# Stores and reloads of a streaming softmax kernel on two issuing queues instead of one

## The chip, the core and the metric

The kernel runs on one core of one Trainium2 chip. The metric is the device time of one execution in microseconds (us), taken as the median of several runs. Beside the times there is a profile of one execution: a trace of each engine's instructions and of the DMA transfers, and a page that sums it up. The engines that matter here are VectorE (DVE in the profile), ScalarE (ACT) and SyncE (SP). SyncE computes nothing; it issues DMAs. A name with a q behind it (SPq, ACTq, DVEq) is the instruction sequencer of that engine, which waits on semaphores and issues DMAs.

## What is computed

```python
B, H, S = 2, 8, 2112
rel = pos[:, None] - pos[None, :]
bias = rel_bias[:, np.clip(rel, -16, 16) + 16]      # H x S x S
logits = logits + bias[None]
exp = np.exp(logits - logits.max(axis=-1, keepdims=True))
return exp / exp.sum(axis=-1, keepdims=True)
```

It is a row softmax over a 2 x 8 x 2112 x 2112 float32 tensor, with a bias that depends only on the distance between row and column. All 285 MB of the input are read once and all 285 MB of the output are written once.

## The kernel before, in words

The tensor has B·H·S = 33792 rows of 2112 numbers. Each of the 128 partitions owns 264 rows that follow one another in memory (`ROWS`). They are worked through in 44 **chunks** of 6 rows (`R = 6`), so that one chunk is 128 partitions x 12672 numbers, 6336 KB. Four buffers `X[0]` to `X[3]` (`NBUF`) take the chunks in turn, chunk n in buffer n mod 4, and everything happens in place in the buffer. In the text below, L(n) is the load of chunk n, S(n) its store.

Each engine has its own program, and they meet only through semaphores:

- **VectorE** (loop at L191): for each chunk `add` (L162) waits for the load (`ld[b]`), then adds the bias row by row and takes the row's minimum of the negated sum, one instruction per row, and counts up `added`. Then `scale` (L180) waits in two halves of three rows for the exponentials (`expd`), takes reciprocals, multiplies each row and counts up `scaled`. `add` of the next chunk starts only after `scale` of this one, since it is one program.
- **ScalarE** (loop at L197): `exps` (L171) waits for `added` row by row and does one exponential with its sum per row.
- **SyncE** issues every load and every large store (L86 to L92, L203 to L214). It begins with six one-row loads of chunk 0, then L(1), L(2), L(3). Then comes S(0), and a loop whose step for chunk j is: wait until chunk j+1 is scaled, issue S(j+1), wait until S(j) has landed (`st[b]`), issue L(j+4) into the buffer that has come free. The last three chunks are stored behind the loop, the last one in two halves of three rows. `take` (L73) is the wait on a semaphore that also counts it down again.

Loads and stores thus stand in one queue, in the order S(j+1), L(j+4), S(j+2), L(j+5). One load or store is spread over the core's 16 DMA engines, eight partitions to each.

The set-up before the loops (L96 to L156) builds the bias lookup `M` once; the change does not touch it. ScalarE issues one small DMA there, for the bias table (L97).

Of the kernel before, what the change touches and what calls it, by code (L numbers as in the profile page):

```python
# [11 lines left out]
ENG = mybir.EngineType  # L12
# [3 lines left out]
def kernel(  # L16
# [6 lines left out]
    nc = tc.nc  # L23
# [5 lines left out]
    ROWS = B * H * S // P  # L29
    PB = S // ROWS  # L30
    assert ROWS * P == B * H * S and PB * ROWS == S and PB == H == 8
    R = 6
    NBUF = 4
    STEP = R * NBUF
    N = ROWS // R
    HALF = R // 2
# [6 lines left out]
    X = [io.tile([P, R * S], FP32, tag=f"X{b}", name=f"X{b}") for b in range(NBUF)]  # L43
# [9 lines left out]
    def view(t, offset, dims):  # L53

        return bass.AP(tensor=t.tensor, offset=t.offset + offset, ap=[[list(t.ap[0])[0], P]] + dims)

    def rows(t, j, n):

        return bass.AP(tensor=t.tensor, offset=t.offset + j * S, ap=[[ROWS * S, P], [1, n * S]])

    with tc.tile_critical(no_gpsimd_drain=True):
        ld = [nc.alloc_semaphore(f"ld{b}") for b in range(NBUF)]
        st = [nc.alloc_semaphore(f"st{b}") for b in range(NBUF)]
# [9 lines left out]
        def take(eng, sem, n):  # L73
            eng.wait_ge(sem, n).then_inc(sem, -n)  # L74


        def load(j, b):
            nc.sync.dma_start(out=X[b][:, :], in_=rows(logits, j, R)).then_inc(ld[b], 16)

        def store(j, b, s0=0, n=R):  # L80
            take(nc.sync, scaled, n)
            nc.sync.dma_start(
                out=rows(out, j + s0, n), in_=X[b][:, s0 * S : (s0 + n) * S]
            ).then_inc(st[b], 16)


        for r in range(R):
            nc.sync.dma_start(
                out=X[0][:, r * S : (r + 1) * S], in_=rows(logits, r, 1)
            ).then_inc(ld[0] if r == R - 1 else pre, 16)  # L90
        for n in range(1, NBUF):
            load(n * R, n)  # L92

# [2 lines left out]
            out=rbB,  # L98
            in_=bass.AP(tensor=rel_bias.tensor, offset=rel_bias.offset, ap=[[0, P], [1, H * W]]),
# [27 lines left out]
        for m, op in ((eq, ALU.is_equal), (gt, ALU.is_gt), (le, ALU.is_le), (lt, ALU.is_lt)):  # L127
# [4 lines left out]
            out=view(F, 0, [[W, H], [1, W]]), in0=view(F, 0, [[W, H], [1, W]]),  # L132
# [9 lines left out]
            out=view(F, 0, [[W, PB], [1, W]]), in0=view(F, SC + 2 * PB, [[1, PB], [0, W]]),  # L142
# [7 lines left out]
            out=view(M, U, [[ROWS, PB], [1, W]]), in0=view(F, 0, [[W, PB], [1, W]]),  # L150
            in1=view(F, SC + 8 * PB, [[1, PB], [0, W]]), op=ALU.add))
        then(v.tensor_copy(out=view(M, U + W, [[ROWS, PB], [1, ROWS - W]]),  # L152
                           in_=view(F, SC + 7 * PB, [[1, PB], [0, ROWS - W]])))
# [14 lines left out]
                    op0=ALU.add, op1=ALU.min, accum_out=nmax[:, r : r + 1],  # L168
                ).then_inc(added, 1)

        def exps(b):  # L171
            for r in range(b * R, (b + 1) * R):
                x = X[b][:, (r - b * R) * S : (r - b * R + 1) * S]
                take(nc.scalar, added, 1)
                nc.scalar.activation(  # L175
                    out=x, in_=x, func=EXP, scale=-1.0, bias=nmax[:, r : r + 1],
                    accum_out=tot[:, r : r + 1],
                ).then_inc(expd, 1)

        def scale(b):  # L180
            for r0 in range(b * R, (b + 1) * R, HALF):
                take(v, expd, HALF)
                v.reciprocal(out=rec[:, r0 : r0 + HALF], in_=tot[:, r0 : r0 + HALF]).then_inc(inv, 1)  # L183
                take(v, inv, 1)
                for r in range(r0, r0 + HALF):
                    x = X[b][:, (r - b * R) * S : (r - b * R + 1) * S]
                    v.tensor_scalar_mul(out=x, in0=x, scalar1=rec[:, r : r + 1]).then_inc(scaled, 1)  # L187
# [3 lines left out]
        with nc.Fori(0, ROWS - STEP + 1, STEP, engines=[ENG.DVE]) as j:  # L191
            strip(j)
            take(v, dve, 1)
            for b in range(NBUF):
                add(b)
                scale(b)
        with nc.Fori(0, ROWS // STEP, 1, engines=[ENG.Activation]):  # L197
            for b in range(NBUF):
                exps(b)

        store(0, 0)  # L203
        with nc.Fori(0, ROWS - 2 * STEP + 1, STEP, engines=[ENG.SP]) as j:
            for b in range(NBUF):
                store(j + (b + 1) * R, (b + 1) % NBUF)
                take(nc.sync, st[b], 16)
                load(j + (b + NBUF) * R, b)
        for n in range(N - NBUF + 1, N - 1):
            store(n * R, n % NBUF)  # L210
        store((N - 1) * R, (N - 1) % NBUF, 0, HALF)
        store((N - 1) * R, (N - 1) % NBUF, HALF, R - HALF)
        for b in range(NBUF):
            take(nc.sync, st[b], 32 if b == (N - 1) % NBUF else 16)  # L214


# [28 lines left out]
```

## Time and profile before

| | us |
|---|---|
| time, median of 3 runs (lowest to highest) | 1329.75 (1329.24 to 1329.9) |
| span of the profiled execution, first to last instruction | 1327.7 |
| median less span (what lies around the span) | 2.05 |
| VectorE busy | 976.6 |
| ScalarE busy | 575.2 |
| bytes moved by DMA | 571.11 MB |

The profiled execution's own device time is not listed apart from its span; the three times lie within 0.66 us of each other, so the span with 2.05 us around it is used for it. How to read the views: the page gives each engine's busy time and share, what the DMA queues moved, and for each kind of DMA issue the median time from issue to landing. The timeline has one line per instruction (or per run of alike instructions): its start, its duration, its engine and program line, the operation with the tensors it writes and reads, and behind "x" how many. The view by windows gives busy times of each engine between two points in time, and as its last two columns the mean busy share of the 16 DMA engines and the rate in GB/s. The view of the waits says which engine waited for what, how long in total, how often, and the longest.

### The profile page before, as it was taken

What the parts mean: (1) busy time and instruction counts of PE and PEld (TensorE: products, weight loads), DVE (VectorE), ACT (ScalarE), POOL (GpSimd) and SP (SyncE); (2) the same over time, 40 slices, a digit from 0 to 9 for tenths busy, and PEclk for the clock granted to TensorE, in tenths of its full rate; (3) what the DMA queues carried; (4) which work ended last, traced back from release to release, by engine and by line L of the source; (5) the groups of instructions that cost most, each with busy time, mean ns of one, the idle gap of its engine ahead of it and who ended that gap; (6) DMA issues with size and microseconds to landing.
All of it is one profiled execution on the core that took longest, in us unless ns stands there. A gap on an engine that the chain in (4) does not pass through costs nothing. (4 is left out here: it accounts for less than half of the span.)

```text
span 1327.7 us, 2454 instructions
## 1 busy us (share of the span) xinstructions
DVE 976.6 (74%) x911; ACT 575.2 (43%) x539; POOL 0.4 (0%) x6
## 2 busy tenths in 40 slices
DVE  6999667777777776687778777677877776687772
ACT  2564333444444343345444333444444343335440
POOL 0000000000000000000000000000000000000000
DMA  9999999999999999999999999999999999999998
GB/s 392 431 428 437 435 420 437 435 434 425 435 437 434 428 435 434 435 429 429 438 438 432 426 438 437 437 425 437 437 437 425 435 440 437 428 432 438 437 426 359
DMA packets 13683, 571.11 MB, mean 430 GB/s; under 512 B 1521, under 2 KB 1649, under 8 KB 1649
## 3 DMA queue, kind: packets, MB, share of 16 engines
q1 hardware_dynamic: 13536, 570.96, 99.6%
q10 hardware_dynamic: 144, 0.14, 0.1%
q14 instruction: 3, 0.02, 0.0%
HBM read 285.61 MB, written 285.47 MB: 430 GB/s over the span
## 5 line engine op out<-in xcount | busy, mean ns | idle before, releaser
L166 DVE CUSTOM_DVE_ANT_0 X<-X,F 128x2112 f32<-128x2112 f32 x264 | 605.2, 2354 | 301.3 <-DVEq L74 301.3
L175 ACT ACTIVATE X<-X,nmax 128x2112 f32<-128x2112 f32 x264 | 541.7, 2052 | 539.3 <-ACTq L74 517.6
L187 DVE TENSOR_SCALAR X<-X,rec 128x2112 f32<-128x2112 f32 x264 | 332.4, 1315 | 13.2
L175 ACT ACT_TABLE_LOAD x11 | 14.1, 1283 | 183.3 <-ACTq L74 183.3
L175 ACT ACTIVATION_READ_ACCUMULATOR X<-X,nmax 128x1 f32 x264 | 49.2, 186 | 0.0
L160 DVE COPY F<-M 128x2135 f32 x11 | 26.1, 2374 | 6.3 <-DVEq L74 6.3
L166 DVE DVE_READ_ACCUMULATOR2_ANT nmax<- 128x1 f32 x264 | 21.7, 82 | 0.0
L183 DVE RECIPROCAL rec<-tot 128x3 f32<-128x3 f32 x88 | 14.9, 170 | 0.0
L131 DVE TENSOR_TENSOR F<-F 128x264 f32<-128x264 f32 x1 | 0.4, 434 | 4.7 <-DMA F<-in_rel_bias_dram 4.7
L152 DVE COPY M<-F 128x1848 f32<-128x1848 f32 x1 | 2.1, 2077 | 0.0
L118 DVE TENSOR_SCALAR ip<-ip 128x8 int32<-128x8 int32 x1 | 0.2, 173 | 1.3 <-POOL ip L102 1.3
L135 DVE TENSOR_REDUCE rbS<-F 128x33 f32<-128x264 f32 x1 | 0.6, 610 | 0.0
L149 DVE TENSOR_TENSOR M<-F 128x264 f32<-128x264 f32 x1 | 0.4, 441 | 0.0
L141 DVE TENSOR_TENSOR F<-F,rbS 128x264 f32<-128x264 f32 x1 | 0.4, 425 | 0.0
L128 DVE TENSOR_SCALAR F<-F 128x8 f32<-128x8 f32 x4 | 0.4, 166 | 0.0
L154 DVE COPY M<-rbS 128x247 f32<-128x247 f32 x1 | 0.4, 408 | 0.0
L139 DVE TENSOR_SCALAR F<-F,rbS 128x8 f32<-128x8 f32 x1 | 0.2, 231 | 0.0
L145 DVE SCALAR_TENSOR_TENSOR F<-F,rbS 128x8 f32<-128x8 f32 x1 | 0.2, 225 | 0.0
L140 DVE TENSOR_SCALAR F<-F,rbS 128x8 f32<-128x8 f32 x1 | 0.2, 222 | 0.0
L146 DVE SCALAR_TENSOR_TENSOR F<-F,rbS 128x8 f32<-128x8 f32 x1 | 0.2, 219 | 0.0
L124 DVE TENSOR_TENSOR F<-ip 128x8 f32<-128x8 int32 x1 | 0.2, 167 | 0.0
L121 DVE TENSOR_TENSOR F<-ip 128x8 f32<-128x8 int32 x1 | 0.2, 166 | 0.0
(9 smaller groups left out, 1.2 us busy)
## 6 DMA issues: line engine op xcount, KB each, us to landing
X<-in_logits_dram SPq DMA_DIRECT2D x43, 6336.0 KB, 44.6
out_dram<-X SPq DMA_DIRECT2D x43, 6336.0 KB, 52.6
X<-in_logits_dram SPq DMA_DIRECT2D x6, 1056.0 KB, 12.1
out_dram<-X SPq DMA_DIRECT2D x2, 3168.0 KB, 21.1
F<-in_rel_bias_dram ACTq DMA_DIRECT2D x1, 132.0 KB, 6.2
```

The lines of the kernel that those rows point to most:

```text
L128: then(v.tensor_scalar(out=m, in0=dp, scalar1=0.0, scalar2=None, op0=op))
L131: then(v.tensor_tensor(out=view(F, 0, [[W, H], [1, W]]), in0=view(F, 0, [[W, H], [1, W]]), in1=view(F, SC + 3 * PB, [[1, H], [0, W]]), op= ...
L135: then(v.tensor_reduce(out=rbS[:, :], in_=view(F, 0, [[1, W], [W, H]]), axis=mybir.AxisListType.X, op=ALU.add))
L141: then(v.tensor_tensor(out=view(F, 0, [[W, PB], [1, W]]), in0=view(F, SC + 2 * PB, [[1, PB], [0, W]]), in1=view(rbS, W - 1, [[0, PB], [-1, ...
L149: then(v.tensor_tensor(out=view(M, U, [[ROWS, PB], [1, W]]), in0=view(F, 0, [[W, PB], [1, W]]), in1=view(F, SC + 8 * PB, [[1, PB], [0, W]] ...
L152: then(v.tensor_copy(out=view(M, U + W, [[ROWS, PB], [1, ROWS - W]]), in_=view(F, SC + 7 * PB, [[1, PB], [0, ROWS - W]])))
L154: then(v.tensor_copy(out=M[:, 0:U], in_=low.to_broadcast([P, U])))
L160: v.tensor_copy(out=F[:, :], in_=M[:, bass.ds(ROWS - STEP - j, FW)]).then_inc(dve, 1)
L166: v.tensor_tensor_reduce(out=x, in0=x, in1=F[:, STEP - 1 - r : STEP - 1 - r + S], scale=-1.0, scalar=BIG, op0=ALU.add, op1=ALU.min, accum_ ...
L175: nc.scalar.activation(out=x, in_=x, func=EXP, scale=-1.0, bias=nmax[:, r : r + 1], accum_out=tot[:, r : r + 1],).then_inc(expd, 1)
L183: v.reciprocal(out=rec[:, r0 : r0 + HALF], in_=tot[:, r0 : r0 + HALF]).then_inc(inv, 1)
L187: v.tensor_scalar_mul(out=x, in0=x, scalar1=rec[:, r : r + 1]).then_inc(scaled, 1)
```

## The change

All loads but the first two chunks' move from SyncE's queue to ScalarE's. ScalarE issues L(2) and L(3) right behind the first row's exponential of chunk 0. In its loop the step for chunk j is: the exponentials of chunk j+1, then a wait until S(j) has landed, then the issue of L(j+4). SyncE's loop is left with the stores alone: wait until chunk j is scaled, issue S(j). The last two chunks (42 and 43) are stored in halves, where before only chunk 43 was. VectorE's program is the same in both kernels.

```diff
-        def load(j, b):
-            nc.sync.dma_start(out=X[b][:, :], in_=rows(logits, j, R)).then_inc(ld[b], 16)
+        def load(eng, j, b):
+            eng.dma_start(out=X[b][:, :], in_=rows(logits, j, R)).then_inc(ld[b], 16)
...
-        for n in range(1, NBUF):
-            load(n * R, n)
+        load(nc.sync, R, 1)
...
-        def exps(b):
-            for r in range(b * R, (b + 1) * R):
+        def exps(b, first=0, last=R):
+            for r in range(b * R + first, b * R + last):
...
-        with nc.Fori(0, ROWS // STEP, 1, engines=[ENG.Activation]):
+        exps(0, 0, 1)
+        for n in range(2, NBUF):
+            load(nc.scalar, n * R, n)
+        exps(0, 1, R)
+        with nc.Fori(0, ROWS - 2 * STEP + 1, STEP, engines=[ENG.Activation]) as j:
             for b in range(NBUF):
-                exps(b)
-        store(0, 0)
+                exps((b + 1) % NBUF)
+                take(nc.scalar, st[b], 16)
+                load(nc.scalar, j + (b + NBUF) * R, b)
+        for n in range(N - NBUF + 1, N):
+            exps(n % NBUF)
         with nc.Fori(0, ROWS - 2 * STEP + 1, STEP, engines=[ENG.SP]) as j:
             for b in range(NBUF):
-                store(j + (b + 1) * R, (b + 1) % NBUF)
-                take(nc.sync, st[b], 16)
-                load(j + (b + NBUF) * R, b)
-        for n in range(N - NBUF + 1, N - 1):
+                store(j + b * R, b)
+        for n in range(N - NBUF, N - 2):
             store(n * R, n % NBUF)
-        store((N - 1) * R, (N - 1) % NBUF, 0, HALF)
-        store((N - 1) * R, (N - 1) % NBUF, HALF, R - HALF)
+        for n in range(N - 2, N):
+            store(n * R, n % NBUF, 0, HALF)
+            store(n * R, n % NBUF, HALF, R - HALF)
         for b in range(NBUF):
-            take(nc.sync, st[b], 32 if b == (N - 1) % NBUF else 16)
+            take(nc.sync, st[b], 32 if b >= NBUF - 2 else 16)
```

## The prediction

> **What bounds the kernel now.** I read the page first, then the waits, then SyncE's timeline, then windows. The page says that no compute engine is near full and that the DMA engines are:
>
> ```profile
> span 1327.7 us, 2454 instructions
> DVE 976.6 (74%) x911; ACT 575.2 (43%) x539; POOL 0.4 (0%) x6
> ...
> DMA packets 13683, 571.11 MB, mean 430 GB/s; under 512 B 1521, under 2 KB 1649, under 8 KB 1649
> q1 hardware_dynamic: 13536, 570.96, 99.6%
> ...
> X<-in_logits_dram SPq DMA_DIRECT2D x43, 6336.0 KB, 44.6
> out_dram<-X SPq DMA_DIRECT2D x43, 6336.0 KB, 52.6
> X<-in_logits_dram SPq DMA_DIRECT2D x6, 1056.0 KB, 12.1
> out_dram<-X SPq DMA_DIRECT2D x2, 3168.0 KB, 21.1
> ```
>
> One queue holds the DMA engines for 99.6% of the span. Its 94 issues (43 + 43 + 6 + 2) make 13536 packets, 144 each: on each of 16 engines 8 rows and one more packet for the semaphore. The waits point the same way: SyncE waits nearly throughout, and VectorE's largest wait is for loads.
>
> ```profile
> SPq L74 <- SPq L74: 1273.1, 87, 36.9
> ...
> DVE X L166 <- DVEq L74: 301.3, 41, 8.8
> ```
>
> SyncE's timeline gives the beat. L78 is a load, L82 a store; each load from the one at 81.12 on is issued at the moment at which a store has landed on all 16 engines.
>
> ```profile
> 4.36 1.74 SPq L78 DMA_DIRECT2D X<-in_logits_dram  x3
> 43.07 22.23 SPq L82 DMA_DIRECT2D out_dram<-X  x2
> 81.12 0.36 SPq L78 DMA_DIRECT2D X<-in_logits_dram  x1
> ...
> 126.28 0.35 SPq L78 DMA_DIRECT2D X<-in_logits_dram  x1
> 133.23 0.34 SPq L82 DMA_DIRECT2D out_dram<-X  x1
> ...
> 579.19 0.35 SPq L78 DMA_DIRECT2D X<-in_logits_dram  x1
> ...
> 1237.05 0.35 SPq L78 DMA_DIRECT2D X<-in_logits_dram  x1
> ```
>
> From 126.28 to 579.19 there are 15 periods of 30.19 us, from 579.19 to 1237.05 there are 22 of 29.90 us. The late beat is steady, and one load and one store take half of it each, 14.95 us, if they cost the same. When a load is issued, the load before it and one store are still queued, about 30 us of work, and it lands 44.6 us later. So the queue never runs dry: this kernel is bound by transfers, end to end. Windows confirm it and show the edges:
>
> ```profile
> 0.00:2.00 2.00, 0.63 (x5) 0.00 (x0) 0.42 (x6) 1.00 0.00 2
> ...
> 126.00:428.00 302.00, 219.09 (x203) 130.02 (x123) 0.00 (x0) 1.00 1.00 433
> ...
> 934.00:1237.00 303.00, 225.61 (x209) 134.80 (x128) 0.00 (x0) 1.00 1.00 434
> ...
> 1320.00:1328.00 8.00, 0.00 (x0) 0.00 (x0) 0.00 (x0) 1.00 0.27 114
> ```
>
> The last two columns are the DMA engines' mean busy share and the rate. Early and late windows differ by about 1 GB/s in the mean over 16 engines, though the beat differs by 0.29 us in 30 (1%). So the early loss falls on some engines only, and the beat follows the slowest. Its sum is 15 x 0.29 = 4.35 us. The last window shows the same lag at the end: 0.27 x 8 = 2.2 us of work per engine, while the last store lands over 6 us into it. By the late beat the loss has stopped, once some engines trail the others. My reading is that it arises where all engines turn from load to store together; the rows don't prove the cause.
>
> **The change, part by part.** Bytes: both kernels move the same 571.11 MB in the same rows, so the 29.90 us of a load and a store stay, if two queues are served at the rate of one. What could differ is whether an engine ever has nothing to do, and what a row costs.
>
> *Hold on ScalarE.* The new wait for S(j) stands ahead of L(j+4) and of all later exponentials. Behind it on ScalarE are exps(j+2), behind those VectorE's scaling of chunk j+2, then S(j+2). Its price is read from the first chunk (a row of exponentials, the scaling, the next chunk's first add) and the second:
>
> ```profile
> 24.94 2.06 ACT L175 ACTIVATE X<-X,nmax 128x2112 f32<-128x2112 f32 x1
> ...
> 37.10 0.19 ACT L175 ACTIVATION_READ_ACCUMULATOR X<-X,nmax 128x1 f32 x1
> 38.87 0.17 DVE L183 RECIPROCAL rec<-tot 128x3 f32<-128x3 f32 x1
> 39.19 3.78 DVE L187 TENSOR_SCALAR X<-X,rec 128x2112 f32<-128x2112 f32 x3
> 42.88 2.35 DVE L166 CUSTOM_DVE_ANT_0 X<-X,F 128x2112 f32<-128x2112 f32 x1
> ...
> 56.76 2.06 ACT L175 ACTIVATE X<-X,nmax 128x2112 f32<-128x2112 f32 x1
> ...
> 64.58 2.35 DVE L166 CUSTOM_DVE_ANT_0 X<-X,F 128x2112 f32<-128x2112 f32 x1
> ```
>
> Six exponentials in a row take 37.29 - 24.94 = 12.35 us; from the reciprocal to the store's issue is 43.07 - 38.87 = 4.2 us; a DMA issue is 0.35 us (SyncE's, taken for ScalarE's). So S(j+2) can be issued 0.4 + 12.35 + 4.2 = 17.0 us after S(j) has landed. The adds of chunk j+2 are out of the way by then: chunk j+1 was released one beat earlier, so VectorE was free at 17.0 - 29.9 = -12.9 us, and adds last 13.9 us (42.88 to 56.76). At S(j)'s landing the engines still have S(j+1) and the new L(j+4), 14.95 + 14.95 = 29.9 us. S(j+2) comes 12.9 us before they run dry, whatever order the two queues are served in. Cost: 0 on the path; if that cover were gone, each us past 29.9 would be a us per beat.
>
> *Loads.* L(j+4) is needed when VectorE gets to chunk j+4, 29.9 + 17.0 = 46.9 us after S(j)'s landing. Alone it takes 14.95 us, beside a store at half rate 29.9 us, plus what is left of L(j+3). It is 17 us early. VectorE's 301.3 us of waiting for loads shrink and turn into waits for exponentials, which is worth nothing, as VectorE doesn't set the end.
>
> *Start.* L(2) and L(3) are issued behind the first exponential, at 24.94 to 27.0 us, instead of at 5 us. L(1) covers that:
>
> ```profile
> L78 SPq DMA_DIRECT2D X<-in_logits_dram x2: 537/600/664, 4.4 to 4.9; - x2
> ...
> DMA to landing us min/median/max: 31.2/38.6/46.0
> ```
>
> L(1), issued at 4.4, lands at 35.6 us, over 8 us after the new issue. Two issues on ScalarE take 0.8 us and delay S(0) by at most that, while L(2) and L(3) run. Cost 0; gain 0, since S(0) merely shares with loads that ran ahead of it before. SyncE's loop loses its waits and load issues, also worth 0: it was waiting.
>
> *Tail.* Loads no longer stand behind stores, so less store work may be left to cover the last compute. Count from S(39)'s landing, which releases L(43) and exps(41). Compute: S(41) at 17.0; chunk 42 takes 64.58 - 42.88 = 21.7, so 38.7; chunk 43 another 21.7, so its second half is issued at 60.4 and its first 4 us before, at 56.4 us. Transfers: L(43), S(40), S(41), S(42), 4 x 14.95 = 59.8 us. An issue at 0.92 to 0.97 moved nothing until 2.00 in the first window, so about 1 us to the first byte. Margin 59.8 - 57.4 = 2.4 us: no gap, but thin. Halving chunk 42 adds one issue of 0.34 us off the path and gains nothing: engines get to S(42) at 3 x 14.95 = 44.9 us, when it has been whole since 38.7. Halving chunk 43 was there before.
>
> *What a row costs with two queues at once.* No row of before shows this. Served a whole transfer at a time, an engine turns from load to store once a period as now; served row by row, 8 times. One turn costs the slowest engine 0.29 us (early beat less late beat) or 0 (late beat). The late beat holds for 22 of 37 periods, and with engines out of step, as they would be with mixed queues; I take 0. Below nothing it can go as far as the early loss goes away, -4.35 us. Above, 7 more turns in 43 periods are 301 turns: at 0.29 us, 87 us; at the mean engine's early loss (433 against 434 GB/s is about 0.07 us a period), 21 us.
>
> On the order of service, the Trainium skill (DMA: Bandwidth & Descriptors, "Queues, rings and completion order") says that each DMA engine goes round-robin between queues with work and changes only at packet boundaries. That would be the row-by-row end, eight turns: the sum stays at zero price and is 1351 us at 0.07 us. No row here shows two bulk queues together.
>
> Sum: 1327.7 + 2.05 around it + 0 + 0 + 0 + 0 = 1329.75, the median of the runs; I say **1329.5**.
>
> **The rivals.**
> (A) *The lag never builds.* Two queues break up the common turn from load to store, the early beat becomes 29.90 too: 1329.75 - 4.35 = **1325.4**. For: the loss exists and ended without any rest in traffic. Against: the engines start in step in both kernels, so it may build up all the same. Against A stands the Trainium skill (DMA: Bandwidth & Descriptors, "Issuing engines are not separate DMA queues"): several issuing engines save only issue time; by that alone the time stays 1329.75, and the steady 434 GB/s agrees that there is little to win.
> (B) *Turns cost in every period.* Place: the DMA engines, wherever both queues hold rows. Price as above, 21 us by the mean engine: **1351**, up to 1417. It decides against the kernel from 2.7 us / 301 = 9 ns a turn. For: early beats show turns that cost. Against: 22 later periods show turns at 0.
> (C) *A gap in the tail.* If compute there takes over 2.4 us longer than counted (the hold delays chunk 41, say), the engines stand idle ahead of S(43). With 3 to 6 us over, **1333**.
> That the split does nothing since the queue was always full is my forecast itself.
>
> **How the numbers follow.** Forecast 40% (1327.2 to 1332.3, its own range), A 25% (1323.5 to 1327), B 28% (1333 to 1417), C 7% (1332.5 to 1336). A measurement of this kernel can tell about 0.2%, 2.66 us, from no change. Faster 0.25 is A; same 0.40 the forecast; slower 0.35 is B and C. From 1323.5 to 1352 holds all but half of B (14%) and a few per cent at the low end.
>
> **What would show it.** On the new page: two queues with about half the bytes each, the rate still 434 GB/s in mid-run windows, stores landing some 45 us and loads 30 us or more after issue. The beat between stores: 29.9 us throughout speaks for A, 30.2 early and 29.9 late for the forecast, over 30.3 all along for B. ScalarE should wait at its line 74 for stores, VectorE for exponentials rather than loads. For C, a window behind the last load with a DMA share well below 1 ahead of the last drain. If the DMA share falls in mid-run, my count of the hold on ScalarE is wrong.

## The result, and the profile after

The changed kernel takes 1335.68 us (median of 22 runs, 1327.48 to 1337.58) against 1330.12 us of the kernel before (22 runs beside it on the same chip, 1328.92 to 1333.13). The ratio is 1.0027, 95% interval 1.0015 to 1.0039: slower by about 0.3%, and clear of the noise. (The ratio is worked out from the single runs, so it isn't the quotient of the two medians, 1.0042.) What is new is the scatter. The old kernel's runs lie within 4.2 us, the new one's within 10.1 us, with 5 of 22 under 1331 us and 13 over 1334 us. The profiled run is one of the long ones: 1337.58 us, span 1335.8 us, so 1.8 us lie around the span. Ratios, here and below, leave out runs more than 1.5% above the fastest of their kernel.

The page of the changed kernel, the lines that answer to those shown of before:

```profile
span 1335.8 us, 2464 instructions
DVE 981.2 (73%) x911; ACT 545.8 (41%) x529; POOL 0.4 (0%) x6
...
DMA packets 13826, 571.11 MB, mean 428 GB/s; under 512 B 1536, under 2 KB 1664, under 8 KB 1664
q1 hardware_dynamic: 7632, 298.45, 51.8%
q10 hardware_dynamic: 6192, 272.64, 47.3%
...
X<-in_logits_dram ACTq DMA_DIRECT2D x42, 6336.0 KB, 37.5
out_dram<-X SPq DMA_DIRECT2D x42, 6336.0 KB, 42.6
```

The change did what it says: two queues with about half of the bytes each. A load and a store take 37 and 43 us from issue to landing. That alone doesn't show how the queues are served, since waiting in one queue made it 45 and 53 us before. The packets do: the kept trace lists each DMA packet (one for each row; a row is one partition's 50,688 bytes of a chunk) with its queue, start and duration, and on one engine a packet starts within a few ns of the end of the one before. So the neighbours on an engine can be found: 2886 load rows are followed by a store row, 3025 store rows by a load row. The engines serve both queues together, row by row. The Trainium skill (DMA: Bandwidth & Descriptors, "Queues, rings and completion order") has each engine go round between its queues, and these packets agree. The waits of the changed kernel:

```profile
ACT X L174 <- ACTq L74: 721.4, 42, 19.3
DVE rec L182 <- DVEq L74: 304.5, 80, 7.8
...
DVE X L165 <- DVEq L74: 5.5, 12, 2.1
```

VectorE waited 301.3 us for loads before; now it waits 304.5 us for exponentials and 5.5 us for loads. Idle time has moved from one wait to another. It isn't what makes the time: the same transfers without any computation take as long (e4 below). The end shows what does. Windows of the changed kernel:

```profile
934.00:1237.00 303.00, 226.36 (x206) 126.79 (x123) 0.00 (x0) 1.00 1.00 432
1308.00:1313.00 5.00, 4.79 (x7) 2.97 (x4) 0.00 (x0) 1.00 0.09 41
1314.00:1328.00 14.00, 2.86 (x3) 0.00 (x0) 0.00 (x0) 1.00 0.99 422
1330.00:1334.00 4.00, 0.00 (x0) 0.00 (x0) 0.00 (x0) 1.00 0.06 25
```

In mid-run the engines are busy. From 1308 to 1313 us, ahead of the last chunk's stores, the share is 0.09, and in the last 4 us it is 0.06. One engine of 16 is 0.0625. So in the end **one DMA engine works while fifteen are done**, and it also works through the gap in which the fifteen stand idle. It has fallen behind the others. When it fell behind is seen in the issues of loads on ScalarE's timeline, each of which follows a store's landing on all 16 engines and so keeps the slowest engine's time:

```profile
23.65 0.83 ACTq L78 DMA_DIRECT2D X<-in_logits_dram  x2
...
107.02 0.35 ACTq L78 DMA_DIRECT2D X<-in_logits_dram  x1
...
714.94 0.34 ACTq L78 DMA_DIRECT2D X<-in_logits_dram  x1
...
867.00 0.34 ACTq L78 DMA_DIRECT2D X<-in_logits_dram  x1
...
1256.26 0.34 ACTq L78 DMA_DIRECT2D X<-in_logits_dram  x1
```

There are 38 beats from 107.02 to the last, 1256.26. At the old late beat of 29.90 us they would take 1136.2 us; they take 1149.2, so 13.0 us are lost. The first 25 beats (to 867.00) take 30.40 us each and lose 12.5 us of it, the last 13 take 29.94 us.

The packets show where that time goes. A row usually takes 1.872 us. 75 of the 10880 whole rows take over 2.0 us (**long rows** below), up to 2.92 us, and 64 of these are load rows. Of the 64, 56 stand directly ahead of a store row on their engine; of the 1534 load rows that stand directly ahead of another load row, none is long. Followed back from the last packet to about 50 us, the late engine never pauses, and its rows take 13.3 us more than 1.872 us each. Of this, 12.3 us lie in load rows directly ahead of a store row, 30 of 281 of which are long. The other fifteen engines lose 0.5 to 4.5 us each. So the late engine is late because some of its load rows at a turn from load to store take longer.

### The profile page after: what moved, and what is told of

It reads as the page before. It is cut to its first block, busy times and chain, and to the rows that moved or that the text cites. A ratio compares the mean times of both kernels' runs of the same rounds, so it can differ in the third digit from the quotient of the medians.

```text
span 1335.8 us, 2464 instructions
## 1 busy us (share of the span) xinstructions
DVE 981.2 (73%) x911; ACT 545.8 (41%) x529; POOL 0.4 (0%) x6
## 5 line engine op out<-in xcount | busy, mean ns | idle before, releaser
L182 DVE RECIPROCAL rec<-tot 128x3 f32<-128x3 f32 x88 | 15.5, 176 | 304.5 <-DVEq L74 304.5
```

## The experiments

Times are medians; ratios are to runs of the kernel before beside them. The theory after the first profile: one DMA engine falls behind in mid-run, wherever two queues of loads and stores are served together (**lag**). Rivals: a gap in the tail made by the hold on ScalarE or by late compute (**tail**), the traffic of VectorE and ScalarE, and the number of turns from load to store.

**e1: the changed kernel again.** No edit.

> The changed kernel once more, unaltered, for a second profile. Theory (lag): the end is set by one of the 16 DMA engines, which falls behind in the middle of the run because some of its rows take longer; the other 15 idle ahead of the last chunk and at the end. Then the span is about 1321 us plus that engine's lag, and a run with a shorter span has a shorter stretch at the end in which the DMA share is 1/16 = 0.06. Rival (tail gap): the end is late because the last chunk's stores are not ready when all engines have drained; then every run has the same idle stretch of 6 us ahead of the last store and the span is near 1335 us each time.

One run, 1337.19 us, span 1335.4 us. The same shares at the end, but lost at another time. Its load issues:

```profile
107.03 0.35 ACTq L78 DMA_DIRECT2D X<-in_logits_dram  x1
...
707.09 0.34 ACTq L78 DMA_DIRECT2D X<-in_logits_dram  x1
...
1255.87 0.34 ACTq L78 DMA_DIRECT2D X<-in_logits_dram  x1
```

Here the first 20 beats take 30.00 us and the last 18 take 30.49 us; in the first profile it was 30.40 and 30.07 us (split at 714.94). In these two profiles the loss falls in different parts of the run and comes to the same sum. As the span was not shorter, this run alone doesn't decide between lag and tail.

**e2: queues swapped.** Stores move to ScalarE's queue, ahead of the next exponentials; loads to SyncE's (`store` then issues on `nc.scalar`). No exponential waits for a landing.

```diff
             for b in range(NBUF):
+                store(j + b * R, b)
                 exps((b + 1) % NBUF)
-                take(nc.scalar, st[b], 16)
-                load(nc.scalar, j + (b + NBUF) * R, b)
...
+                take(nc.sync, st[b], 16)
+                load(nc.sync, j + (b + NBUF) * R, b)
```

Chunk 42 is stored whole in it, and L(2) and L(3) are issued at the start.

> Stores on ScalarE's queue (each ahead of the next chunk's exponentials), loads on SyncE's queue behind the wait for the store; so still two queues served together, but no exponential waits for a store to land any more, and L(2) and L(3) are issued at the start. Theory (lag from two queues served together): about as slow as the changed kernel, 1330 to 1338 us, with one or a few engines trailing by 5 to 15 us. Rival (the hold on ScalarE starves the tail): without the hold the last chunk is ready at least 10 us earlier, no idle stretch ahead of it, 1325 to 1330 us.

1332.21 us (12 runs, 1327.87 to 1337.4), ratio 1.0019 (1.0004 to 1.0034). Without any hold the long runs are as long as the changed kernel's (1337.4 against 1337.6). The profiled run was a short one, span 1326.7 us, and has no gap ahead of the last chunk:

```profile
1308.00:1313.00 5.00, 0.00 (x0) 0.00 (x0) 0.00 (x0) 1.00 1.05 451
```

That doesn't show that the swap took the gap away, since a short run with the hold has none either (e8). What decides is the time of the long runs: the hold is not what makes them. The rival *tail* is out as their cause.

**e3 and e4: transfers alone.** Additions, exponentials and scaling are left out, so the output is the logits; a store waits for its load. e3 keeps the one queue and its order, e4 the two queues; both store the last chunks whole.

```diff
-            take(nc.sync, scaled, n)
+            take(nc.sync, ld[b], 16)
...
-        with nc.Fori(0, ROWS - STEP + 1, STEP, engines=[ENG.DVE]) as j:
-            strip(j)
...
```

> The kernel before without additions, exponentials and scaling: loads and stores alone, in the old order on the one queue; a store waits for its load, so the output is the logits. Theory (transfers alone make the lag): the beat and the trailing stretch are as in the kernel before, about 1325 to 1329 us. Rival (VectorE's and ScalarE's SBUF traffic stretches the rows): no lag, about 1322 us.

> The changed kernel without additions, exponentials and scaling: loads on ScalarE's queue, stores on SyncE's, chunk stores whole; the output is the logits. Theory (two queues served together make the lag grow larger, whatever the engines compute): 3 to 10 us slower than the copy on one queue, with one engine trailing. Rival (the hold or the compute does it): the same as the copy on one queue within 2 us.

e3: 1331.35 us (10 runs, 1329.48 to 1332.93), ratio 1.0007 (0.9998 to 1.0016). e4: 1336.97 us (4 runs, 1333.63 to 1337.62), ratio 1.0043 (1.0028 to 1.0058). e3 lies above both of its expectations, e4 is slower than e3 by 5.6 us, as the theory had it. The end of e4 has the signature, with one to two engines busy:

```profile
1330.00:1334.00 4.00, 0.00 (x0) 0.00 (x0) 1.00 0.09 38
```

By its packets e4 has two late engines, which lose 12.5 and 12.0 us. Both the old kernel's time and the loss are there without a compute instruction in the loops. The engines' traffic in SBUF makes neither.

**e5 and e6: other orders on one queue.** e5 issues two stores, then two loads, and so halves the turns. e6 cuts each transfer into halves of three rows and alternates them, and so doubles the turns.

```diff
 # e5
-            for b in range(NBUF):
+            for b in range(0, NBUF, 2):
-                store(j + (b + 1) * R, (b + 1) % NBUF)
-                take(nc.sync, st[b], 16)
-                load(j + (b + NBUF) * R, b)
+                store(j + (b + 1) * R, (b + 1) % NBUF)
+                store(j + (b + 2) * R, (b + 2) % NBUF)
+                for c in (b, b + 1):
+                    take(nc.sync, st[c], 16)
+                    load(j + (c + NBUF) * R, c)
 # e6
+                for h in range(2):
+                    half_store(j + (b + 1) * R, (b + 1) % NBUF, h)
+                    take(nc.sync, sth[h][b], 16)
+                    half_load(j + (b + NBUF) * R, b, h)
```

> The kernel before with its one queue in another order: two stores, then two loads (S(j+1), S(j+2), L(j+4), L(j+5)), so that the engines turn from load to store half as often. Theory (each turn from load to store stretches the last rows on some engines until they trail): half the turns, about half of the 4 to 6 us of lag, 1326 to 1328 us. Rival (the lag grows with time or with load rows, whatever the order): as before, 1329 to 1331 us. Third possibility (the deeper order starves the queue): over 1332 us with a DMA share below 1 in mid-run.

> The kernel before with every load and store cut into two halves of three rows, and halves of loads and stores in turn on the one queue, so twice as many turns and no second queue. Theory (turns make the lag): larger lag than before, 1333 to 1338 us. Rival (two queues served at once are needed for it): as before within 2 us, 1328 to 1332 us.

e5: 1334.31 us (11 runs, 1332.44 to 1336.48), ratio 1.0028 (1.0019 to 1.0037): slower, though it has half the turns. Its DMA share stays at 1.00 while the rate falls, so in mid-run the engines never ran dry; the rows themselves took longer:

```profile
126.00:428.00 302.00, 219.15 (x203) 131.09 (x123) 0.00 (x0) 1.00 1.00 434
934.00:1237.00 303.00, 222.67 (x204) 132.43 (x124) 0.00 (x0) 1.00 1.00 428
```

Its packets show which. It has 185 long rows. Of these 154 are in the second load of a pair, which stores follow, 115 of them its last row; the first load, which another load follows, has 2.

e6: 1333.01 us (11 runs, 1332.67 to 1333.82), ratio 1.002 (1.0011 to 1.0029), just inside the theory's 1333 to 1338 us. Its late beat speaks against the theory all the same:

```profile
768.02 0.35 SPq L90 DMA_DIRECT2D X<-in_logits_dram  x1
...
1217.89 0.35 SPq L90 DMA_DIRECT2D X<-in_logits_dram  x1
```

That is 30 half-loads, 15 periods of 29.99 us against 29.90: a fixed 0.09 us for the two added transfers of a period, with no growing loss, and the runs lie within 1.2 us of each other. Earlier, from 120.85 to 423.14, ten periods take 30.23 us each: the loss comes early and stops, as in the old kernel. So the long rows stand at turns from load to store, but not every turn costs the same: one price per turn fits neither e5 nor e6.

**e7 and e14: one direction at a time.** All loads, then all stores, nothing computed, the output not meaningful; e7 on SyncE's queue, e14 with even chunks on SyncE's queue and odd ones on ScalarE's, a loop of this form on each.

```diff
 # e7
+                take(nc.sync, ld[b], 16)
+                load(j + (b + NBUF) * R, b)
...
+                take(nc.sync, st[b], 16)
+                store(j + (b + NBUF) * R, b)
```

> All 44 loads on SyncE's queue, then all 44 stores, no computation, the output is not meaningful: the same bytes with one turn only. Theory (turns or a mix of both directions make rows slower): no engine trails by more than 1.5 us, beat 14.95 us in both parts, 1322 to 1325 us. Rival (one engine or one address range is slow in loads by itself): the trailing stretch builds in the first half, 1328 us or more.

> All loads, then all stores, no computation, the output is not meaningful; even chunks from SyncE's queue, odd chunks from ScalarE's, so that two queues are served together but always in one direction. Theory (an engine falls behind only where loads run beside stores): no lag over 2 us, 1327 to 1332 us, as loads then stores on one queue. Rival (two queues served together are enough): an engine trails by 5 us or more, 1334 us and above.

e7: 1329.99 us (10 runs, 1329.89 to 1330.25), ratio 0.9994 (0.9984 to 1.0003). e14: 1326.0 us (5 runs, 1325.74 to 1326.13), ratio 0.9965 (0.9952 to 0.9978). Neither scatters by more than 0.4 us. Both miss the theory's ranges, e7 above (1322 to 1325 us) and e14 below (1327 to 1332 us), but not by lag. The windows at e7's one turn, then the same windows of e14:

```profile
660.00:668.00 8.00, 0.00 (x0) 0.00 (x0) 1.00 0.68 291
660.00:668.00 8.00, 0.00 (x0) 0.00 (x0) 1.00 1.00 431
```

In e7 the engines stand idle for 0.32 x 8 = 2.6 us, as its first store waits for all loads; in e14 one queue bridges the other's wait. e7 has no long row at all; e14 has 17, of which 15 lie in its first 100 us, and no engine loses over 2.2 us. So e14 decides between the two theories: two queues served together lose nothing where both load or both store. The loss needs loads beside stores.

**e8 and e10: chunk 42 whole.** The halves of chunk 42 alone are undone; e10 is the same kernel timed beside e9, the changed kernel once more.

```diff
-        for n in range(N - NBUF, N - 2):
+        for n in range(N - NBUF, N - 1):
             store(n * R, n % NBUF)
-        for n in range(N - 2, N):
-            store(n * R, n % NBUF, 0, HALF)
-            store(n * R, n % NBUF, HALF, R - HALF)
+        store((N - 1) * R, (N - 1) % NBUF, 0, HALF)
+        store((N - 1) * R, (N - 1) % NBUF, HALF, R - HALF)
```

> The changed kernel with chunk 42 stored in one piece again. By the prediction's tail sum and by the lag theory: no difference to the changed kernel, 1330 to 1338 us with its scatter. Rival (the halves of chunk 42 cover a gap in the tail): slower than the changed kernel by 2 to 4 us in every run, so none under 1331 us.

> The changed kernel unaltered, timed beside the others of this call on the same chip, with a third profile. Lag theory: single runs scatter from 1327 to 1338 us, never above about 1338; the span less the lag of the last engine is the same in all profiles, about 1321 to 1323 us.

> The changed kernel with chunk 42 stored whole, timed on the same chip as the changed kernel. If the halves of chunk 42 are worth nothing either way, the two medians differ by less than their scatter lets one tell (about 3 us). If the halves cost something, this kernel stays near 1329 us while the changed kernel is near 1335 us.

e8: 1329.04 us (10 runs, 1327.75 to 1337.58, six of them under 1331 us, where the rival had none), ratio 1.0008 (0.9989 to 1.0026). On another chip, side by side, e9: 1335.51 us (12 runs, 1328.29 to 1337.73), ratio 1.0014 (0.9995 to 1.0032), and e10: 1334.11 us (12 runs, 1327.85 to 1337.12), ratio 1.0016 (1.0001 to 1.0031). There the changed kernel's interval takes in no change at all. The kernel with chunk 42 whole gives 1329.04 and 1334.11 us by how many of its runs are long, and the halves can't be told from the whole. e8's profiled run was a short one, span 1326.0 us, and is the counterpart to the changed kernel's. Its load issues:

```profile
106.98 0.35 ACTq L78 DMA_DIRECT2D X<-in_logits_dram  x1
...
856.09 0.34 ACTq L78 DMA_DIRECT2D X<-in_logits_dram  x1
...
1245.84 0.34 ACTq L78 DMA_DIRECT2D X<-in_logits_dram  x1
```

and its end:

```profile
1308.00:1313.00 5.00, 0.00 (x0) 0.00 (x0) 0.00 (x0) 1.00 1.02 441
1322.00:1326.00 4.00, 0.00 (x0) 0.00 (x0) 0.00 (x0) 1.00 0.03 13
```

Here 38 beats take 29.97 us, there is no gap ahead of the last chunk, and by 1326 us all is done. The last load is issued 10.4 us earlier than in the changed kernel's profile (1245.84 against 1256.26), and the span is 9.8 us shorter. Nearly all that sets a long run apart from a short one has happened by then, in the slowest engine's beat.

One thing that e1 and e9 had expected did not come: the span less the trailing stretch at the end is not about 1321 to 1323 us in every profile. In the long profiles of the changed kernel (e9's as well as the first) one engine trails by some 5.3 us at the end, which leaves over 1330 us; the fifteen others had to wait up to 6.6 us more ahead of the last chunk.

**e11: two queues, each with loads and stores in turn**, transfers alone, the output the logits: even chunks on SyncE's queue, odd ones on ScalarE's, so with two buffers to a queue (`first` is 0 on SyncE, 1 on ScalarE).

```diff
+                for b in (first, first + 2):
+                    store(j + (b + 2) * R, (b + 2) % NBUF)
+                    take(eng, st[b], 16)
+                    load(j + (b + NBUF) * R, b)
```

> Loads and stores alone, no computation, the output is the logits: two queues again, but each with loads and stores in turn (even chunks on SyncE's queue, odd chunks on ScalarE's). Theory (one engine falls far behind because loads and stores stand in separate queues, so that it goes on loading while the others only store): small lag as with one queue, 1328 to 1332 us. Rival (any two queues served together do it): 1334 to 1338 us as the copy on two queues.

1370.23 to 1425.71 us in 4 runs, outside both expectations. Its windows:

```profile
100.00:500.00 400.00, 0.00 (x0) 0.00 (x0) 1.00 1.00 434
700.00:1300.00 600.00, 0.00 (x0) 0.00 (x0) 1.00 0.92 387
```

It begins at full rate; later the engines are idle 8% of the time, so it also starves, and its time doesn't say how much is lag. It doesn't separate what it was meant to.

**e12 and e13: six buffers of four rows** in place of four of six (R = 4, NBUF = 6), in the changed kernel and in the one before.

> The changed kernel with six buffers of four rows instead of four of six rows, so that more loads are outstanding; 132 transfers instead of 88. Theory (the lag feeds itself in the stretches in which the other engines have no load left): with loads always queued the lag stays small, 1324 to 1329 us with 2 us for the added transfers. Rival (the lag comes from two queues as such): 1330 to 1338 us, scattered as the changed kernel.

> The kernel before (one queue) with six buffers of four rows, 132 transfers. Theory (more and shorter transfers outstanding in two queues keep the engines in step; in one queue the lag is that of the kernel before): 5 us of lag again, 1330 to 1334 us. Rival (the shorter transfers alone remove the stretched rows): no lag, 1326 to 1329 us, as the better runs of six buffers on two queues or faster.

e12: 1329.51 us (12 runs), a little above the theory's 1324 to 1329 us. Eight of its runs lie between 1329.21 and 1329.60 us, and the ratio, 0.9988 (0.9979 to 0.9998), is theirs; four lie between 1352 and 1362 us. The profile is of one of the eight, and 2 of its 16512 whole rows take more than 7% longer than the usual 1.251 us, though loads run beside stores in it: two queues need not lose. No profile of the other four was seen, so what they are stays open, and as it stands this version is no gain. e13: 1330.99 us (11 runs, 1330.58 to 1331.77), ratio 1.0005 (0.9996 to 1.0014): as the theory had it, the shorter transfers alone bring nothing on one queue.

## Why the prediction was wrong, point by point

- **What bounds it: right.** Transfers do, in both kernels, and the time is that of the slowest of the 16 engines. The lag that the prediction read from the old beat (4.35 us) is of the same kind as what decides the changed kernel, and its reading of the place holds: 77 of the old profile's 85 long rows are the last row of a load, at the turn to the store. But there seven engines lose 3.4 to 5.2 us each, and the loss stops; here it is one engine.
- **Hold on ScalarE: right, at price 0.** From S(39)'s landing to the store of chunk 41 the sum was 17.0 us. In the changed kernel's timeline the landing releases L(43) at 1256.26; the last scaling of chunk 41 ends at 1269.68 + 3.78 = 1273.46, 17.2 us after. The first row is the issue of L(42), the last one the last scaling of chunk 43:

```profile
1226.42 0.34 ACTq L78 DMA_DIRECT2D X<-in_logits_dram  x1
...
1256.26 0.34 ACTq L78 DMA_DIRECT2D X<-in_logits_dram  x1
...
1269.68 3.78 DVE L186 TENSOR_SCALAR X<-X,rec 128x2112 f32<-128x2112 f32 x3 [0.15 <-DVEq L74]
...
1313.09 3.78 DVE L186 TENSOR_SCALAR X<-X,rec 128x2112 f32<-128x2112 f32 x3
```

- **Loads and start: right.** VectorE's waits for loads went (5.5 us left) and were worth nothing. L(2) is issued at 23.65 us, a little earlier than counted, as ScalarE's sequencer issues it before the first exponential runs (24.86 us).
- **Tail: the sum was right, the reading of it incomplete.** Compute came as counted: the last scaling ends at 1316.87, 60.6 us after S(39)'s landing (60.4 forecast). The gap that rival C described is there, but for fifteen engines only (3.8 to 6.6 us by the packets). They had run ahead of the one whose landing starts the count; for that one the margin held. From S(39)'s landing it has 5 x 14.95 = 74.75 us of transfers and what is left of L(42) (issued at 1226.42, landed 37.1 us later at 1263.5, so 7.3 us at half share, 3.6 us), together 78.4 us, which gives 1334.6. The last half is issued when its scaling ends, and 1316.87 + 17.7 is 1334.6 as well. The slowest engine had no pause; it was late. The two landings, from the view of the DMA issues (KB each, us to landing):

```profile
X<-in_logits_dram ACTq DMA_DIRECT2D x1, 6336.0 KB, 37.1
...
out_dram<-X SPq DMA_DIRECT2D x1, 3168.0 KB, 17.7
```

- **Halves of chunk 42: right** that they bring nothing that can be measured (e9, e10).
- **What a row costs with two queues at once: wrong, and this is the step that failed.** The prediction took 0 for a turn from load to store, since the old late beat showed turns at 0. On the late engine the turns cost 12.3 us over the 281 counted, 0.044 us each, five times the 9 ns from which rival B decides against the kernel. On the fifteen others it is 10.3 us over 2578 turns, 0.004 us each. So B had the place right, and its price of 21 us on all engines wrong: the rate in mid-run is 432 GB/s, 434 before, and one engine pays 13.0 us by the beat. Nor is it one price for every turn: most cost nothing, doubling them on one queue gave no growing loss (e6), halving them was slower (e5). The loss appears where loads run beside stores (e4), and not with two queues in one direction (e14); on one queue it stays at 4 to 7 us on the slowest engine in e3, e6 and e13 (e5 loses on all engines, for a reason that stays open).
- **The forecast was met by some runs, A by none.** 8 of the 22 runs lie in the forecast's 1327.2 to 1332.3 us, none in A's 1323.5 to 1327. The median, 1335.68, fits the ranges of B and C, but neither price: B's was on all engines, C's gap was to come from late compute. What no case held is that one and the same program would do either: a draw from run to run between a loss of a few us and some 13 us. The forecast put its weight on a single likeliest time.

**What stays open.** Why a load row ahead of a store row sometimes takes longer, why mostly on one engine, which engine it is (the trace doesn't name it), and why the loss ends at about the same sum: the two profiles shown reach the last load at 1256.26 and 1255.87 us after losing time in different parts of the run. That the fifteen others, once a chunk ahead, have less queued and so disturb it less is a guess. No run tried it, but the packets fit it: in the three long profiles of the changed kernel (the first, e1, e9), 6 of the late engine's 232 load rows are long while no other engine loads, and 78 of 755 while some other does.

## What to carry to other kernels

When transfers bound a kernel, the time is that of the slowest DMA engine and not the mean rate: look at the last microseconds in windows, where a DMA share of 1/16 names a single late engine, and at the beat of the issues that wait for landings. Moving loads and stores to separate queues removes waits that look large in the profile (here 300 us on VectorE) and gains nothing if the engines were never short of work; it also lets them run loads beside stores, and that made this kernel's time a draw. Profile such a version more than once and look at the single runs before a median is believed.

## What the runs showed of the hardware that was not expected

- **The time is lost at the turn from load to store, on few engines.** Most long rows are load rows directly ahead of a store row: 77 of 85 in the old kernel, nearly all on seven engines, and 56 of 75 in the changed one, about half of them on one engine. In the four long profiles (the changed kernel, e1, e9, e10) none of 3405 load rows ahead of another load row is long. Most turns cost nothing: nine engines of the old kernel's profile lose at most 0.6 us each.
- **Long transfers in one direction, one queue against two.** All loads then all stores take 1329.99 us on one queue and 1326.0 us on two (e7, e14). Of these 4.0 us, 2.6 are e7's pause at its one turn. The loads gain nothing, 1.876 us for a row in both; a row of a store takes 1.878 us in e7 and 1.873 in e14. The Trainium skill (DMA: Bandwidth & Descriptors, "Issuing engines are not separate DMA queues") says that issuing from several engines saves only what it takes to initiate a DMA, and that this is small beside the DMA itself; the loads agree. That the two queues can also cost 13 us, when one loads and the other stores, the runs add to it.
- **Even "the same kernel" has two medians.** Ten and twelve runs of one program, on two chips, gave 1329.04 and 1334.11 us (e8, e10), by how many of the runs were long.
